# Nineteen projection panels with channels in rows, and a new order of the input projection, in a one-core hybrid decoder layer

## The chip, the cores and the metric

The kernel runs on one core of a Trainium2 chip. TensorE (PE in the profile; its weight loads are a row of their own, PEld) multiplies; VectorE (DVE), ScalarE (ACT) and GpSimd (POOL) do the work on elements; SyncE (SP) issues all transfers. The metric is the time of one execution in microseconds (us) on the device: the median of the runs of a kernel. Lower is better.

## What is computed

One layer over 256 tokens of 1024 channels, all in float32. Cut to what matters here:

```python
h = rms_norm(x, ln1_g)
q, k, v, z, xbc, dt_raw, gate_a, gate_b = split(h @ w_in)      # 1024 x 10272
y_a = attention(rms_norm(q), rms_norm(k), v) @ w_o_attn        # 16 heads of 64, causal
xs, bm, cm = split(silu(conv4(xbc) + conv_b))                  # conv along tokens, per channel
dt = softplus(dt_raw + dt_bias); a = dt * -exp(a_log)          # 32 heads, 4 groups
y = y_diag + y_off + d_skip * xs                               # two chunks of 128 tokens
#   y_diag: (C B^T) * exp(segsum(a)) @ (xs dt);  y_off: (C @ state of chunk 0) * exp(cumsum(a))
y_b = (rms_norm_by_group(y * silu(z)) * ssm_norm_g) @ w_o_ssm
x = x + (sigmoid(gate_a) * y_a + sigmoid(gate_b) * y_b) @ w_out
h2 = rms_norm(x, ln2_g)
g_ff, u_ff = split(h2 @ w_gate_up)
x = x + (silu(g_ff) * u_ff) @ w_down
x = x + (p @ w_ple_proj) * sigmoid(rms_norm(x, ln3_g) @ w_ple_gate)
```

## The kernel before

Every big product runs in *panels* of 512 weight columns by 1024 rows. A panel's weights come in four transfers of 128x1024 (two k rows of 512 columns each) into `raw`; ACT rounds them to `wh` and DVE subtracts to get the rest, `wl` (`split_w`, L260 to L263). The activations are split in the same way into a high and a low part, so a product is three matmuls in the fp32r type: high by `wh`, high by `wl`, low by `wh`.

In a `Panel` (L333) the activations are stationary and the weights move: for each of two token tiles and eight k rows three matmuls of 512 columns (`step`, L365), 48 in all, into two PSUM banks of the tag `g`. The result has tokens in rows. What is used with channels in rows is turned back by PE: `evac_xbc` (L499) and `evac_z` (L533) copy the two banks out with the token's `rstd` as scale and transpose them in eight 128x128 blocks; `evac_gu` and `ff_task` (L1016, L1026) form silu(gate) times up in token rows and transpose four blocks. The activations carry the gain of the norm but not its rstd, which is applied when a panel is copied out.

`dt_task` (L416) forms dt from sixteen small fp32r matmuls and writes the decays; `e1`, the decay from a chunk's start, has tokens in rows. In `ssm_task` (L608) four groups are worked in two halves of four heads: `decay_rows` fills rows by POOL and by transfers on SP (L639, L640), `prep` makes the group's operands, `seg` the decay matrices, `out_` (L681) the products within a chunk, `off` (L697) the product with the state: one F32 matmul of 512 columns, a DVE product with `e1`, and four transposes.

PSUM has four banks `g` for panels and four `b` (`pb`) for all else. The buffers of SBUF are pools: `s4` 26, `s2` 8, `raw` 4, `wh` 3, `wl` 6.

What runs in which order on PE is set by a planner in the program, `Filler` (L78): tasks are generators that yield a due time in ns of planned PE time, from the table `LAG` (L68); after each step of a panel the earliest due task may put its instructions behind it. `queue` (L156) fixes this order on PE. On ACT, DVE and SP the order comes from priorities (`prio`: weights before copies out before background) in a scheduler. `PANELS` (L34) is the order of the input projection; the weights lie in that order in DRAM, and SP loads them in a row.

## Time and profile before

| | us |
|---|---|
| median of 3 runs | 602.09 (601.91 to 602.18) |
| span of the profiled execution | 600.7 |
| PE busy | 593.9 (99%) |
| PE weight loads (beside PE) | 484.6 (81%) |
| DVE busy | 424.1 (71%) |
| ACT busy | 338.6 (56%) |
| POOL busy | 38.7 (6%) |

Busy time of PE is modelled from the records of its pipelined matmuls, so the price of one is read from the distance between starts. The input projection with attention and SSM runs to about 345 us, the output projection and the residual to 395, the eleven gate and up panels to 520, the down projection to 580, the last panels to the end.

### The profile page before, as it was taken

What the parts mean: (1) busy time and instruction counts of PE and PEld (TensorE: products, weight loads), DVE (VectorE), ACT (ScalarE), POOL (GpSimd) and SP (SyncE); (2) the same over time, 40 slices, a digit from 0 to 9 for tenths busy, and PEclk for the clock granted to TensorE, in tenths of its full rate; (3) what the DMA queues carried; (4) which work ended last, traced back from release to release, by engine and by line L of the source; (5) the groups of instructions that cost most, each with busy time, mean ns of one, the idle gap of its engine ahead of it and who ended that gap; (6) DMA issues with size and microseconds to landing.
All of it is one profiled execution on the core that took longest, in us unless ns stands there. A gap on an engine that the chain in (4) does not pass through costs nothing.

```text
span 600.7 us, 8147 instructions
## 1 busy us (share of the span) xinstructions
PE 593.9 (99%) x2965; PEld 484.6 (81%) x2965; DVE 424.1 (71%) x668; ACT 338.6 (56%) x513; POOL 38.7 (6%) x47
## 2 busy tenths in 40 slices
PE   8999999999999999999999999999999999999997
PEld 7888888787777878887787788888888888888886
DVE  5689999978997765677875475756756666646465
ACT  6766666556775545576646444755544544445353
POOL 2000103412010011101000000000000000000000
PEclk9999999999999999999999999999999999999999
DMA  8945644533444445555544475556565555555641
GB/s 278 323 152 175 210 142 142 174 131 117 140 127 149 143 150 170 187 166 160 162 161 164 139 232 188 185 165 208 163 200 188 161 201 187 190 188 182 201 141 70
DMA packets 31192, 103.88 MB, mean 173 GB/s; under 512 B 3568, under 2 KB 4912, under 8 KB 31152
## 3 DMA queue, kind: packets, MB, share of 16 engines
q1 hardware_dynamic: 31152, 103.36, 53.3%
q8 instruction: 23, 0.38, 0.3%
q14 instruction: 17, 0.14, 0.1%
HBM read 102.23 MB, written 1.05 MB: 172 GB/s over the span
## 4 chain that ended last, share of the span: by engine, by line
PE 96%; DVE 1%; DMA 1%; ACT 0%; SPq 0%; issue 0%; ACTq 0%
PE g L170 85%; PE pb L170 6%; PE pb L192 5%; DMA raw<-in_head 1%; SPq L248 0%; DVE s L750 0%; ACT wh L151 0%; DVE s L658 0%; ACT s L151 0%; DVE wl L263 0%; DVE s L785 0%; DVE s L663 0%; DVE s L742 0%; DVE s L1063 0%; DVE s L1064 0%
## 5 line engine op out<-in xcount | busy, mean ns | idle before, releaser
L170 PE MATMUL g<-wh,s 128*128 128x512 f32 (+1 forms) x1508 | 486.7, 395 | 0.6 <-ACT wh L151 0.6
L170 PEld LDWEIGHTS g<-wh,s 128*128 128x128 f32 x1508 | 282.7, 189 | 59.6 <-issue 1.8
L263 DVE TENSOR_TENSOR wl<-raw,wh 128x1024 fp32r<-128x1024 f32 (+2 forms) x193 | 230.4, 1196 | 129.6 <-ACT wh L151 127.0
L151 ACT ACTIVATE wh<-raw 128x1024 fp32r<-128x1024 f32 (+2 forms) x193 | 199.9, 1038 | 177.7 <-PE g L170 149.8
L170 PE MATMUL g<-wl,s 128*128 128x512 f32 (+1 forms) x754 | 294.2, 392 | 0.0
L170 PEld LDWEIGHTS g<-wl,s 128*128 128x128 f32 x754 | 142.1, 189 | 27.8 <-issue 1.0
L151 ACT ACTIVATE s<-pb 128x512 f32<-128x512 f32 (+4 forms) x64 | 33.6, 544 | 30.4 <-PE pb L192 16.1
L192 PEld LDWEIGHTS pb<-ident,s 128*128 128x128 f32 x302 | 37.9, 140 | 11.4 <-issue 0.9
L192 PE MATMUL pb<-ident,s 128*128 128x128 f32 x302 | 47.1, 272 | 0.0
L151 ACT ACTIVATE s<-g,rstd 128x512 f32<-128x512 f32 (+1 forms) x50 | 28.5, 583 | 20.5 <-PE g L170 18.7
L520 DVE SCALAR_TENSOR_TENSOR s<-pb,vecs,s 128x255 f32<-128x255 f32 (+2 forms) x72 | 32.0, 475 | 1.4 <-ACT s L151 1.2
L170 PE MATMUL pb<-s,s 128*64 128x128 f32 (+6 forms) x328 | 32.6, 304 | 0.4 <-ACT s L151 0.4
L151 ACT ACTIVATE s<-pb,vecs 128x256 f32<-128x256 f32 (+2 forms) x48 | 25.9, 550 | 11.1 <-PE pb L192 5.0
L170 PEld LDWEIGHTS pb<-s,s 128*64 128x64 f32 (+2 forms) x328 | 23.1, 154 | 9.9 <-issue 4.7
L381 POOL TENSOR_TENSOR rstd<-tiny,mhalf 128x2 f32<-128x2 f32 x3 | 2.3, 762 | 315.2 <-DVE tiny L380 295.3
L151 ACT ACTIVATE s<-s 128x512 f32<-128x512 f32 (+3 forms) x24 | 19.0, 792 | 4.3 <-DVE s L978 4.0
L571 POOL TENSOR_TENSOR tiny<-tiny,mhalf 128x8 f32<-128x8 f32 x8 | 16.0, 1995 | 73.2 <-DVE tiny L569 73.2
L635 POOL TENSOR_SCALAR_AFFINE_SELECT rr<-a_h 128x512 fp32r<-128x512 f32 x16 | 13.6, 860 | 100.2 <-PE pb L170 61.7
L151 ACT ACTIVATE s<-s,tiny 128x128 f32<-128x128 f32 (+1 forms) x32 | 14.2, 444 | 6.5 <-DVE tiny L788 6.5
L1022 DVE SCALAR_TENSOR_TENSOR s<-g,rstd,s 128x256 f32<-128x256 f32 x22 | 10.6, 481 | 7.5 <-ACT s L151 7.5
L676 DVE TENSOR_TENSOR s<-s,s 128x512 f32<-128x512 f32 x16 | 11.9, 748 | 0.3 <-ACT s L151 0.3
L1023 DVE SCALAR_TENSOR_TENSOR s<-g,rstd,s 128x256 f32<-128x256 f32 x22 | 10.7, 484 | 0.7
(120 smaller groups left out, 235.2 us busy)
## 6 DMA issues: line engine op xcount, KB each, us to landing
raw<-in_w_big SPq DMA_DIRECT2D x176, 512.0 KB
raw<-in_head SPq DMA_DIRECT2D x4, 512.0 KB
s<-in_xk SPq DMA_DIRECT2D x4, 512.0 KB
raw<-in_head SPq DMA_DIRECT2D x7, 256.0 KB
raw<-in_w_pp SPq DMA_DIRECT2D x2, 512.0 KB
raw<-in_w_dn SPq DMA_DIRECT2D x2, 512.0 KB
out<-s SPq DMA_DIRECT2D x3, 256.0 KB
xraw<-in_head SPq DMA_DIRECT2D x2, 256.0 KB
```

The source lines that it names most:

```text
L151: return nc.scalar.activation(o, i, f, **kw)
L170: ins = nc.tensor.matmul(o, lhsT, rhs, start=start, stop=stop).ins
L192: queue(nc.tensor.transpose(o, i, ident[: i.shape[0], : i.shape[0]]).ins, False)
L263: nc.vector.tensor_sub(wl, raw, wh.bitcast(F32))
L381: nc.gpsimd.tensor_tensor(dst, t, mhalf[:, : ss.shape[-1]], op=ALU.pow)
L520: stt(cc[:, sft:], pu[:, j, : T - sft], cw[3 - sft], cc[:, sft:], op0=ALU.mult, op1=ALU.add)
L571: nc.gpsimd.tensor_tensor(f, ms, mhalf, op=ALU.pow)
L635: nc.gpsimd.affine_select(r, bcast(a_h[:, c, h0 : h0 + 4].bitcast(F32), P), pattern=[[0, 4], [1, P]], compare_op=ALU.is_ge, fill=0.0, base ...
L676: nc.vector.tensor_tensor(m, m, cbm[:, g, c].unsqueeze(1).to_broadcast([P, 4, P]), op=ALU.mult)
L1022: stt(t[:, tt], pan.ps[tt][:, :T], r, t[:, tt], op0=ALU.mult, op1=ALU.mult)
L1023: stt(t[:, tt], pan.ps[tt][:, T:], r, t[:, tt], op0=ALU.mult, op1=ALU.mult)
```

## The change

*Rows.* The six xbc panels and the nine gate and up panels from the third on use a new class `Rows`: 128 weight columns are stationary, and the normed activations move. High and low part lie side by side, so `wh` is multiplied with 512 columns (high and low at once) and `wl` with 256 (high). A panel is 32 such pairs into four banks `g`, one for each block of 128 channels; ACT copies a bank and DVE adds its two halves. Channels come out in rows, and the transposes go.

*Narrow.* The four z panels do the same with 256 columns three times, 96 matmuls into two banks, which are read in place.

*Norm.* Both need activations that carry their rstd. `norm_task` spreads rstd over rows by one F32 matmul with `ones_m`, scales x and splits it into `hn`; `norm2` does it for h2. The gate panels `ga` and `gb` use `hn` too.

*dt* becomes eight F32 matmuls of 32 stationary columns that go to four quarters of the array's columns. *Decay by loads:* `e1` is made with heads in rows, stored to DRAM, and loaded back in two transfers, spread over 64 rows each. *off* is four F32 matmuls of 128 columns with channels in rows, one DVE product and one sum, with no transposes. *out_* does eight heads of a group in one run, and all decay rows of the next group are filled at once. The two `pow` of a q or k panel become one. `PANELS` and `LAG` are new; `s4` has 22 buffers, `raw` 5, `wh` 4.

```diff
 PANELS = [
+    v0 v1 q0 q1 k1 k0 gb0 xbc5 xbc4 xbc1 xbc2 xbc3 xbc0 z0 z1 z2 z3 gb1 yb0 ga0 yb2 ga1 yb1 yb3
-    xbc4 xbc0 xbc5 xbc1 xbc2 xbc3 k0 q0 z0 z1 gb0 yb0 yb1 q1 v0 z3 k1 z2 gb1 v1 yb2 yb3 ga1 ga0
...
+    class Rows:
+            self.ps = [psg.tile([P, 512], F32, tag="g", name=nm("gr")) for _ in range(4)]
+        def add_all(self, acts, after):
+            for k0 in range(0, 8, 2):
+                if k0 % 4 == 0:
+                    parts = next_chunk()
+                for b in range(4):
+                    cs = slice(b * P, b * P + P)
+                    for k in (k0, k0 + 1):
+                        (wh, wl), hl_ = parts[k % 4], acts[k]
+                            mm(self.ps[b], wh[:, cs], hl_, k == 0, False, main=True)
+                            mm(self.ps[b][:, :T], wl[:, cs], hl_[:, :T], False, k == 7, main=True)
+                    fill.step()
+                    if k0 == 6:
+                        after(b, self.ps[b])
+    class Narrow:
...
+                        for n, (w, a) in enumerate(((wh, ah), (wh, al), (wl, ah))):
+                                mm(o, w[:, cs], a, k == 0 and n == 0 and b % 2 == 0, k == 7 and n == 2 and b % 2 == 1, main=True)
...
+    def norm_task():
...
+            mm(pr[:, :T], ones_m, dg.rearrange("p a t -> p (a t)"), True, True)
...
     def dt_task():
-                mm(pd[:64, :T], wd[:, k].rearrange("p a h -> p (a h)"), ah, k == 0, k == 7)
+            halves(
+                (pd[32 * (k % 4) : 32 * (k % 4) + 32, :T], wdt[:, k], xr_of(k), k < 4, k >= 4)
+                for k in range(8))
...
-            act(e1, pe[:, 3], AF.Exp)
+            act(e1t[:32], pe1, AF.Exp)
+            nc.sync.dma_start(e1d, e1t[:32])
+            for a in range(2):
+                nc.sync.dma_start(e1c[rows_of[a]], e1d.rearrange("(j a) l -> a j l", a=2)[a : a + 1].to_broadcast([64, 16, P]))
...
+    def rows_xbc(i):
+        def after(b, ps):
+                e = s2([512])
+                act(e, ps)
+                nc.vector.tensor_add(u[:, b], e[:, :T], e[:, T:])
+                act(cc, u[:, b], AF.Identity, scale=cw[3], bias=v[:, V_CB + ct : V_CB + ct + 1])
+                for sft in (1, 2, 3):
+                    stt(cc[:, sft:], u[:, b, : T - sft], cw[3 - sft], cc[:, sft:], op0=ALU.mult, op1=ALU.add)
...
         def off(g):
-                mm(po, cb[:, g], xe, True, True)
+                    mm(po[:, i], xe[:, i * P : i * P + P], cb[:, g], True, True)
+                nc.vector.tensor_mul(yo, po, e1c[:, 4 * g : 4 * g + 4])
-                    transpose(pt_[:, i], yo[:, i * P : i * P + P])
-                nc.vector.tensor_add(y[:, :, P:T], y[:, :, P:T], pt_)
+                nc.vector.tensor_add(y[:, :, P:T], y[:, :, P:T], yo)
...
     for i in range(2, NFF):
-        pan = Panel()
-        evac_gu(i, pan)
+        Rows().add_all(h2n, rows_gu(i))
```

Where it moves instructions is shown at three places. On **PE** in the gate and up stage, before, a token tile takes six matmuls of 512 columns into its bank (`g`) for two k rows, three for each, and transposes that belong to the panel before (`s_847` is its product) stand between:

```order
L170 MATMUL g_4130<-wh_4132,s_758_3663 128x512
L170 MATMUL g_4130<-wl_4133,s_758_3663 128x512
L170 MATMUL g_4130<-wh_4132,s_759_3664 128x512
L170 MATMUL g_4130<-wh_4132,s_758_3663 128x512
L170 MATMUL g_4130<-wl_4133,s_758_3663 128x512
L170 MATMUL g_4130<-wh_4132,s_759_3664 128x512
L192 MATMUL pb_4152<-ident,s_847_4122 128x128 x2
L170 MATMUL g_4129<-wh_4138,s_758_3663 128x512
L170 MATMUL g_4129<-wl_4139,s_758_3663 128x512
```

In the changed kernel a block of 128 channels has its own bank (`gr`), the activation (`s_784`) moves, and 512 and 256 columns take turns:

```order
L170 MATMUL gr_4331<-s_796_4145,wh_4391 128x512
L170 MATMUL gr_4331<-s_796_4145,wl_4392 128x256
L170 MATMUL gr_4440<-s_784_4088,wh_4446 128x512
L170 MATMUL gr_4440<-s_784_4088,wl_4447 128x256
L170 MATMUL gr_4440<-s_784_4088,wh_4446 128x512
L170 MATMUL gr_4440<-s_784_4088,wl_4447 128x256
L170 MATMUL gr_4441<-s_784_4088,wh_4446 128x512
L170 MATMUL gr_4441<-s_784_4088,wl_4447 128x256
L170 MATMUL gr_4441<-s_784_4088,wh_4446 128x512
```

The transposes between are gone, and two k rows of a bank are four matmuls in turns of 512 and 256 columns, where they were six of 512.

On **ACT** at the end of a gate and up panel, before, the two copies out of the banks (`s_864<-g`) each stand between roundings of weights (`wh`):

```order
L151 ACTIVATE s_857_4157<-pb_4152 128x512
L151 ACTIVATE s_864_4211<-g_4129,rstd_3511 128x256
L151 ACTIVATE wh_4227<-raw_4226 128x1024
L151 ACTIVATE wh_4265<-raw_4264 128x1024
L151 ACTIVATE s_864_4211<-g_4130,rstd_3511 128x256
L151 ACTIVATE wh_4271<-raw_4270 128x1024
L151 ACTIVATE wh_4310<-raw_4309 128x1024
```

In the changed kernel the four copies out of the banks `gr_4552` to `gr_4555` come at the panel's end, with one `wh` ahead of the last of them:

```order
L151 ACTIVATE wh_4721<-raw_4720 128x1024
L151 ACTIVATE s_895_4640<-gr_4552 128x512
L151 ACTIVATE s_896_4647<-gr_4553 128x512
L151 ACTIVATE s_897_4654<-gr_4554 128x512
L151 ACTIVATE wh_4727<-raw_4726 128x1024
L151 ACTIVATE s_898_4661<-gr_4555 128x512
L151 ACTIVATE s_910_4685<-s_880_4556 128x512
```

Two copies became four, and the fourth is queued behind a rounding of weights.

On **SP** after the weight loads of the first panels, before, only the decay rows (`rr`) stand between loads (`raw`):

```order
L275 DMA raw_1006<-in_w_big 128x1024
L275 DMA raw_1012<-in_w_big 128x1024
L275 DMA raw_1080<-in_w_big 128x1024
L639 DMA rr_831<-low_h 1x4x128
L639 DMA rr_835<-low_h 1x4x128
L640 DMA rr_831<-low_l 1x4x127
L640 DMA rr_835<-low_l 1x4x127
```

In the changed kernel the decay goes out (`e1d<-e1t`) and comes back (`e1c`, two transfers) ahead of the first decay rows:

```order
L277 DMA raw_1109<-in_w_big 128x1024
L277 DMA raw_1115<-in_w_big 128x1024
L569 DMA e1d<-e1t 32x128
L277 DMA raw_1201<-in_w_big 128x1024
L571 DMA e1c<-e1d 64x16x128 x2
L714 DMA rr_1517<-low_h 1x4x128
L277 DMA raw_1207<-in_w_big 128x1024
L715 DMA rr_1517<-low_l 1x4x127
```

The store and the two loads are new in the queue; the weight loads behind them keep their order.

## Rows read from the trace of the kernel before

**Rows 1.** The page: busy time of the engines, the granted TensorE clock in 40 slices (tenths of full speed), and the chain of work that ended last, by engine and by line.

```profile
PE 593.9 (99%) x2965; PEld 484.6 (81%) x2965; DVE 424.1 (71%) x668; ACT 338.6 (56%) x513; POOL 38.7 (6%) x47
...
PEclk9999999999999999999999999999999999999999
...
PE 96%; DVE 1%; DMA 1%; ACT 0%; SPq 0%; issue 0%; ACTq 0%
PE g L170 85%; PE pb L170 6%; PE pb L192 5%; DMA raw<-in_head 1%; SPq L248 0%; DVE s L750 0%; ACT wh L151 0%; DVE s L658 0%; ACT s L151 0%; DVE wl L263 0%; DVE s L785 0%; DVE s L663 0%; DVE s L742 0%; DVE s L1063 0%; DVE s L1064 0%
```

**Rows 2.** The waits of PE in the whole span, by line and by what was waited for: us in total, times, longest us.

```profile
PE pb L205 <- DVE ones L209: 1.1, 1, 1.1
PE g L170 <- ACT wh L151: 0.6, 1, 0.6
PE pb L170 <- ACT s L151: 0.4, 1, 0.4
PE pb L170 <- DVE s L744: 0.3, 1, 0.3
```

**Rows 3.** The timeline of PE in the gate and up stage (start, duration, instruction, how many in a row; durations overlap), and the busy time of the engines over one panel's period of that stage (PE, PEld, DVE, ACT, POOL, granted clock, DMA).

```profile
434.66 0.39 PE L170 MATMUL g<-wh,s 128*128 128x512 f32 x1
434.89 0.38 PE L192 MATMUL pb<-ident,s 128*128 128x128 f32 x2
435.03 0.48 PE L170 MATMUL g<-wh,s 128*128 128x512 f32 x1
435.34 0.39 PE L170 MATMUL g<-wl,s 128*128 128x512 f32 x1
...
436.27 0.62 PE L170 MATMUL g<-wh,s 128*128 128x512 f32 x2
...
436.95 0.61 PE L170 MATMUL g<-wh,s 128*128 128x512 f32 x2
...
416.83:428.22 11.39, 11.39 (x54) 9.36 (x53) 7.35 (x10) 5.68 (x7) 0.00 (x0) 1.00 0.59 192
```

**Rows 4.** The timeline of PE in a stretch of 256-column matmuls near the end, and the weight loads that belong to `wh` in the main groups, with their count and mean duration (ns, before the second bar).

```profile
594.98 0.40 PE L170 MATMUL pb<-wh,s 128*128 128x256 f32 x2
...
595.34 0.40 PE L170 MATMUL pb<-wh,s 128*128 128x256 f32 x2
...
L170 PEld LDWEIGHTS g<-wh,s 128*128 128x128 f32 x1508 | 282.7, 189 | 59.6 <-issue 1.8 <-ACT wh L151 1.0 <-DVE s L572 0.2
```

**Rows 5.** The timeline of PE around dt (the sixteen records at 27.86), around a run of two-way F32 products (204.50) and around an off step (its two records at 214.83 stand between main matmuls, of which one lies between 214.83 and 215.92).

```profile
27.86 2.04 PE L170 MATMUL pb<-s,s 128*64 128x256 f32 x16
29.73 0.40 PE L170 MATMUL g<-wh,s 128*128 128x512 f32 x1
...
204.50 1.09 PE L170 MATMUL pb<-s,s 128*64 128x128 f32 x16
205.53 0.50 PE L170 MATMUL g<-wl,s 128*128 128x512 f32 x1
...
214.60 0.39 PE L170 MATMUL g<-wh,s 128*128 128x512 f32 x1
214.83 1.02 PE L170 MATMUL pb<-s,s 128*128 128x512 f32 x2
...
215.92 0.40 PE L170 MATMUL g<-wl,s 128*128 128x512 f32 x1
```

**Rows 6.** DVE by groups of line, tile and shape: count, busy us, mean ns, idle time before them.

```profile
L263 DVE TENSOR_TENSOR wl<-raw,wh 128x1024 fp32r<-128x1024 f32 x184 | 224.7, 1223 | 126.4 <-ACT wh L151 123.9
...
L520 DVE SCALAR_TENSOR_TENSOR s<-pb,vecs,s 128x255 f32<-128x255 f32 x24 | 11.2, 475 | 1.2 <-ACT s L151 1.2
...
L1022 DVE SCALAR_TENSOR_TENSOR s<-g,rstd,s 128x256 f32<-128x256 f32 x22 | 10.6, 481 | 7.5 <-ACT s L151 7.5
...
L526 DVE SCALAR_TENSOR_TENSOR s<-s,s 128x1024 f32<-128x1024 f32 x6 | 7.3, 1218 | 0.0
...
L744 DVE TENSOR_TENSOR s<-s 128x256 f32<-128x256 f32 x4 | 1.7, 414 | 0.0
```

**Rows 7.** ACT by groups: count, busy us, mean ns, and the idle time before them with what ended it.

```profile
L151 ACT ACTIVATE wh<-raw 128x1024 fp32r<-128x1024 f32 x184 | 194.7, 1060 | 174.5 <-PE g L170 149.8 <-issue 13.0 <-DVE wl L263 3.3
...
L151 ACT ACTIVATE s<-g,rstd 128x256 f32<-128x256 f32 x23 | 10.7, 466 | 9.5 <-PE g L170 9.5
...
L151 ACT ACTIVATE s<-g 128x512 f32<-128x512 f32 x12 | 7.1, 590 | 2.2 <-PE g L170 1.7 <-PE pb L170 0.5
```

**Rows 8.** Busy time of the engines in stretches of the first part (us; PE, PEld, DVE, ACT, POOL, then granted clock, DMA share and GB/s).

```profile
36.00:60.00 24.00, 24.00 (x114) 19.71 (x113) 22.51 (x53) 16.13 (x23) 0.00 (x0) 1.00 0.50 154
60.00:84.00 24.00, 24.00 (x119) 20.16 (x118) 22.84 (x47) 15.05 (x25) 2.45 (x4) 1.00 0.54 176
84.00:108.00 24.00, 23.96 (x116) 19.42 (x114) 22.28 (x39) 16.72 (x24) 8.05 (x6) 1.00 0.47 148
108.00:132.00 24.00, 23.67 (x133) 18.95 (x134) 21.50 (x33) 12.56 (x17) 6.93 (x5) 1.00 0.47 161
```

**Rows 9.** The waits of SP's DMA queue: us in total, times, longest us.

```profile
SPq L275 <- DVE wl L263: 412.0, 163, 7.1
SPq L639 <- POOL rr L635: 24.6, 9, 6.0
...
SPq L1138 <- DMA out<-s: 1.5, 1, 1.5
```

More of the change, by code (lines that the diff above doesn't have):

```diff
@@ L417, in dt_task @@
         with prio("bg"):
-            wdt_raw = s4([8, 32])
-            nc.sync.dma_start(wdt_raw, w_dt)
-            wd = s4([8, 2, 32], F32R)
-            act(wd[:, :, 0], wdt_raw)
-            nc.vector.tensor_sub(wd[:, :, 1], wdt_raw, wd[:, :, 0].bitcast(F32))
+            wdt = s4([8, 32])
+            nc.sync.dma_start(wdt, w_dt)
+            nc.vector.tensor_tensor(wdt, wdt, bcast(g1, 32), op=ALU.mult)
             nc.vector.tensor_scalar(dsk, v[:, V_DS : V_DS + 16], 0.5, None, op0=ALU.mult)
+        while "norm" not in done:
+            yield fill.now + 500
         yield fill.now + LAG["dt"]
@@ L556, in evac_qk, with rows_z, after, end @@
+    def rows_z(i):
+        zs = s4([4, T])
+        def after(jj, ps):
+            zz = zs[:, 2 * jj : 2 * jj + 2]
+            with prio("ev"):
+                act(zz, ps, AF.Tanh, scale=0.5)
+                stt(zz, zz, 1.0, ps, op0=ALU.add, op1=ALU.mult)
+        def end():
+            yield fill.now + LAG["z.end"]
+            zsT[i] = zs
+        return after, end
     def evac_qk(kind, i, pan):
@@ L906, in tile_layer, with split_t @@
             continue
+        if kind in ("xbc", "z"):
+            after, end = (rows_xbc if kind == "xbc" else rows_z)(i)
+            fill.drain(lambda: "norm" in done)
+            if kind == "z":
+                Narrow().add_all(hn_act, after)
+            else:
+                Rows().add_all(hn_rows, after)
+            fill.spawn(end(), 0)
+            continue
+        norm = kind in ("ga", "gb")
+        if norm:
+            fill.drain(lambda: "norm" in done)
         pan = Panel()
         for hf in range(2):
-            pan.add(next_chunk(), h_act[4 * hf : 4 * hf + 4], last=hf == 1)
+            pan.add(next_chunk(), (hn_act if norm else h_act)[4 * hf : 4 * hf + 4], last=hf == 1)
         evacuate(kind, i, pan)
-    def split_t(toks, scale_cols, const_scale, acts, delay):
+    def split_t(toks, scale_cols, const_scale, acts, delay, tiles=None):
         th = s4([4, T], F32R)
         tl = s4([4, T], F32R)
+        if tiles is not None:
+            tiles.append((th, tl))
         yield fill.now + delay
@@ L1037, in ff_task, with norm2 @@
         ff.extend((fh[:, j], fl[:, j]) for j in range(2))
+    h2n = []
+    def norm2():
+        yield fill.now + LAG["n2"]
+        with prio("bg"):
+            dg = s2([2, P])
+            for tt in range(2):
+                act(dg[:, tt], ident, scale=rstd2[:, tt : tt + 1])
+        yield fill.now + LAG["n2.rows"]
+        with prio("bg"):
+            pr = pb([512])
+            mm(pr[:, :T], ones_m, dg.rearrange("p a t -> p (a t)"), True, True)
+            rbc = s2([T])
+            act(rbc, pr[:, :T])
+        for k in range(0, 8, 2):
+            yield fill.now + LAG["n2.k"]
+            th, tl = (res2.tiles[k // 4][m][:, k % 4 : k % 4 + 2] for m in range(2))
+            with prio("bg"):
+                t = s2([2, T])
+                nc.vector.tensor_add(t, th.bitcast(F32), tl.bitcast(F32))
+                nc.vector.tensor_tensor(t, t, rbc.unsqueeze(1).to_broadcast([P, 2, T]), op=ALU.mult)
+                h = s4([2, 2, T], F32R)
+                act(h[:, :, 0], t)
+                nc.vector.tensor_sub(h[:, :, 1], t, h[:, :, 0].bitcast(F32))
+            h2n.extend(h[:, j].rearrange("p a t -> p (a t)") for j in range(2))
@@ new lines, in rows_gu, with after, end @@
+    def rows_gu(i):
+        gu = s4([4, T])
+        def after(b, ps):
+            with prio("ev"):
+                e = s2([512])
+                act(e, ps)
+                nc.vector.tensor_add(gu[:, b], e[:, :T], e[:, T:])
+            if b == 3:
+                fill.spawn(end(), 0, LAG["gu"])
+        def end():
+            with prio("bg"):
+                f = s2([2, T])
+                act(f, gu[:, 0:2], AF.Sigmoid)
+                nc.vector.tensor_mul(f, f, gu[:, 0:2])
+                nc.vector.tensor_mul(f, f, gu[:, 2:4])
+                f2 = s4([2, 2, T], F32R)
+                fh, fl = f2[:, 0], f2[:, 1]
+                act(fh, f)
+                nc.vector.tensor_sub(fl, f, fh.bitcast(F32))
+            yield fill.now + LAG["ff.end"]
+            ff.extend((fh[:, j], fl[:, j]) for j in range(2))
+        return after
@@ L1039, in tile_layer @@
+    fill.spawn(norm2(), 0)
     pair(res2.acts, evac_gu)
-    h2 = res2.acts[0] + res2.acts[1]
+    fill.drain(lambda: len(h2n) == 8)
     for i in range(2, NFF):
-        pan = Panel()
-        for hf in range(2):
-            pan.add(next_chunk(), h2[4 * hf : 4 * hf + 4], last=hf == 1)
-        evac_gu(i, pan)
+        Rows().add_all(h2n, rows_gu(i))
     res3 = Residual(xin, V_G3, rstd3)
```

280 lines of the change are left out of this document (145 added, 135 removed).

## The prediction

> **What bounds the kernel now.** I read the page first. TensorE (PE) is busy 593.9 of 600.7 us, the chain that ended last lies on it for 96% (85% main matmuls into the g banks, 5% transposes), and it was granted the higher level, 2.4 GHz, in all 40 slices [rows 1]. PE's waits for other engines add up to 2.4 us [rows 2]. So the time is the sum of what PE is given to do, and the prediction is a count of instructions multiplied by prices, unless another engine takes the bound over. The profiled execution has a span of 600.7 against the median of 602.09, so 1.4 us lie outside the span; I sum against the span and add them back.
>
> **Prices on PE.** The mean durations of the grouped view overlap (a matmul of 512 columns is listed with 396 ns), so I take distances between starts. Three main matmuls of 512 columns take 436.95 - 436.27 = 0.68 us, 0.227 each [rows 3]. Three of 256 columns take 595.34 - 594.98 = 0.36, 0.120 each, though each has its own load of 128 columns, of 189 ns mean: the load runs beside the stream [rows 4]. A line through both prices is 0.0133 us + 0.417 ns for each column. Two transposes stand between the matmuls that start at 434.66 and 435.03, and the matmul behind them is still late, the next starts at 435.34: 0.68 for two matmuls and two transposes, less 0.453, is 0.227, or 0.113 for a transpose. Over a whole gate and up panel it is 11.39 - 48 x 0.227 = 0.51 for four, 0.127 each [rows 3]. I take 0.12.
>
> **Panels in rows.** Nine gate and up panels and six xbc panels become 32 pairs of 512 + 256 columns each. A pair is 0.227 + 0.120 = 0.347; a panel is 11.09 instead of 48 x 0.2267 = 10.88, or +0.21, times 15 = +3.1 us. The columns are the same in number (24,576); what is added is 16 matmuls, each at 0.0133. Four z panels become 96 matmuls of 256 columns, 11.52 instead of 10.88, +0.64 each, +2.6 us. Together 432 more main matmuls: **+5.7 us**.
>
> Here a page speaks for a better result. The row gives 13 ns for each matmul beyond its columns, from the difference of the 512 and the 256 stream [rows 3, 4]. The Trainium skill, "TensorE: Matmul & The Clock Gate", section "Back-to-back issue gap", states N/2.4 + 2.5 ns for a single matmul at the fast level; by it the 432 added matmuls would cost an estimated 1.1 us instead of 5.7. The trace has 0.227 where it gives 0.216, so the trace decides.
>
> **Transposes.** Xbc loses 48, z 32, gate and up 36 and the off step 16: 132 x 0.12 = **-15.8 us** (14.9 to 16.8 by the two prices). All of them stood on PE between main matmuls, so all of it is path.
>
> **Small steps on PE.** *Off:* the F32 matmul of 512 columns costs 215.92 - 214.60 - 2 x 0.227 = 0.87 [rows 5]; four of 128 columns have as many columns in all: 0 (between -0.3 and +0.3 for each of four groups by what the row of 128-column products leaves open), I take 0. *dt:* the 16 old matmuls take 29.73 - 27.86 = 1.87 [rows 5]. The eight new F32 ones of 256 columns are 0.43 each by half of the off price, 3.4 in series and 0.87 if four quarters of the array run together. The nearest row is a run of eight two-way F32 products of 128 columns (16 records): 205.53 - 204.50 = 1.03, where 8 x 0.87/4 = 1.74 would be the price in series [rows 5]. Two-way sharing thus gives 0.59; I take 1.2 for four-way, **-0.7** (between -1.0 and +1.5). *Norms:* two F32 matmuls of 256 columns with ones_m, 0.43 each and about 0.08 for a change of kind (the matmul behind two transposes is 0.31 - 0.227 late [rows 3]): **+1.0**. *Heads in one run:* four runs of half products instead of eight: -0.2 (0 to -0.4). Sum: 5.7 - 15.8 + 0 - 0.7 + 1.0 - 0.2 = **-10.0 us**.
>
> **What the other engines get.** A Rows panel is copied out by ACT (four copies of 128x512, 0.59 each by the row of today's twelve) and added up by DVE (four 128x256 adds, 0.414) [rows 6, 7]. In the gate and up stage DVE is busy 7.35 and ACT 5.68 of 11.39 [rows 3], so DVE goes to about 7.35 - 4 x 0.48 + 4 x 0.414 and some for the two products, ACT to about 5.68 + 4 x 0.59 - 2 x 0.47 = 7.1: covered by PE. In the six xbc panels DVE is the tight one. A panel asks of it four wl (1.223), twelve conv steps (0.475) and the last product (1.218), 11.8 us by mean durations; the four adds make it 13.5 [rows 6], against 11.1 us on PE. But mean durations overlap on DVE too: in 36 to 132 us it is shown busy 22.51, 22.84, 22.28 and 21.50 of 24 with PE at 24.0, 24.0, 23.96 and 23.67 [rows 8], so PE lost almost nothing while DVE was 90 to 95% busy. The excess of up to 2.4 us a panel has to be carried by the lead of the split weights: six wl buffers of two k rows are worth 6 x 11.09/4 = 16.6 us of PE. Since v, q and k panels come first and z panels behind, where DVE has half a panel free, I count it as carried.
>
> **SP.** The decay round trip puts three transfers into SP's queue between weight loads. The first waits for e1t, the two others for the first to land, and all weight loads behind them wait too; at the end of the program a wait of SP for a transfer to DRAM is 1.5 us, and SP's waits for the split weights are 412 us in 163, at most 7.1: that is slack [rows 9]. Waits of SP for the decay rows are 24.6 us, up to 6.0 each, and no PE wait came of them [rows 2, 9]. The bound for the new stop is 0 to 6.0 + 2 x 1.5 = 9 us on SP, covered by five raw, four wh and six wl buffers (at 2.77 us each, far over 9). I take 0 on PE. The Trainium skill, "DMA: Bandwidth & Descriptors", section "Where the ~2 µs actually goes", puts a transfer's fixed time near 2 us, most of it the write receipt, heaviest for HBM, with the wait on the issuing sequencer. That speaks against a trip out and back, an estimated 4 us on SP; today's 1.5 us is of the same order, and either lies under the lead.
>
> **New waits.** The banks are the other new thing. A Rows panel uses all four g banks and the next panel wants bank 0 again 3 x 0.695 = 2.09 us after its last matmul. ACT copies three blocks, then a wh of 1.06 that was itself waiting for the panel's last matmuls, then the fourth block: 1.06 + 0.59 and some 0.2 for signals is 1.85 of 2.09. It fits with 0.2 us. The new order also shortens leads in the SSM (with the new order priced as above, the shortest is some 2.5 us, ahead of the second group's out step). I add **+0.9 us** for waits of this kind (0 to 4): 600.7 - 10.0 + 0.9 + 1.4 = **593.0 us**. Its own range is 590 to 597.
>
> **The rivals.**
> - *The copies come late.* If the wh ahead of the fourth copy starts later, each of 15 Rows panels stops for 0.3 to 0.5 us: +4.5 to +7.5, 597 to 600.5. For it: the margin of 0.2 us, and ACT's idle time today mostly ends with a PE matmul, that is, its wh is issued just when PE frees the buffer [rows 7]. Against: a fourth wh buffer. Chance 0.12.
> - *DVE becomes the bound and the time gets slower than before.* In the six xbc panels the price by means holds, 6 x (13.5 - 11.1) = 14.4 us, and the lead of 16.6 is already spent on the norm and dt work of the same stretch. It decides as soon as that other work exceeds about 2 us and wl comes late, so PE waits for DVE: 593 + 14 = 607. For it: DVE is at 95% there today [rows 8]. Against: PE was still full at that level. Chance 0.10.
> - *Loads are exposed.* If the 256-column matmul had to wait for its own load of 189 ns, a pair would be 0.227 + 0.189 = 0.416 and the panels +33 us, 626. The 256-column stream with its own loads speaks against it [rows 4]. Chance 0.02.
> - *Added matmuls are nearly free.* If in the alternating stream the 13 ns vanish behind the longer matmul, the 5.7 fall away and the time is 593.0 - 5.7 = 587.3. Against: neither stream of today shows it [rows 3, 4]. Chance 0.04. The Trainium skill's formula of "TensorE: Matmul & The Clock Gate" comes out near it, an estimated 588.4; by the 0.227 of the trace it does not hold here.
>
> **How the numbers follow.** The forecast has 0.72. The range needs 8 in 10: the forecast's 590 to 597 and the late copies up to 600 hold 0.84, and the bounds of dt, off, transposes and waits lie inside, so 590 to 600. About 0.2% (1.2 us) is what a measurement of this kernel can tell from no change. Faster than 600.9: forecast 0.70, free matmuls 0.04, late copies 0.11, together 0.85; within: 0.05, from the tails of forecast, copies and DVE; slower: 0.10, from DVE and exposed loads.
>
> **What would show it.** In the profile after, a gate and up panel should take 11.1 us of PE and a pair 0.347; a z panel 11.5; transposes 171 instead of 303; PE's waits under 4 us, and no wait for ACT's copies at the start of a Rows panel. The forecast is wrong if PE shows waits for ACT s ahead of gr matmuls (the first rival), for DVE wl or the SSM's products before 210 us (the second), or if pairs are at 0.42 or 0.335 (the third and fourth).

## The result and the profile after

The changed kernel takes 596.45 us (median of 4 runs, 595.75 to 597.93) against 602.13 for the kernel before in the same comparison: a ratio of 0.9911, interval 0.9897 to 0.9925. It is 5.7 us faster, where 9.1 was forecast; 596.45 lies in the range of 590 to 600. The profiled execution took 595.75 us, its span is 593.7, so 2.05 us lie outside the span (2.05 to 2.13 in the four runs); runs of the kernel before that list both have 1.7 outside. The prediction added back 1.4, the median of three runs less the span of another one. Of the 3.45 us between 593.0 and 596.45, then, 2.1 lie in the span of the profiled run (593.7 against 591.6), 0.65 outside it, and 0.7 is the distance of the median from that run, the fastest of the four.

The page of the changed kernel, the same lines as in [rows 1]:

```profile
PE 584.9 (99%) x3293; PEld 498.7 (84%) x3293; DVE 452.4 (76%) x733; ACT 360.3 (61%) x562; POOL 38.8 (7%) x44
...
PEclk9999999999999999999999999999999999999999
...
PE 94%; ACT 2%; DVE 1%; issue 1%; POOL 1%; DMA 1%; SPq 0%
PE g L170 50%; PE gr L170 27%; PE gn L170 8%; PE pb L170 7%; PE pb L192 3%; ACT wh L151 1%; ACT s L151 1%; POOL tiny L644 1%; DMA raw<-in_head 1%; DVE wl L265 0%; SPq L250 0%; DVE s L647 0%; DVE s L1120 0%; DVE tiny L640 0%; DVE s L1107 0%
```

PE is as full as before (99%) at the same clock, with 9 us less of busy time. Its share of the chain fell from 96 to 94%: ACT has 2% of it now. The waits of PE, beside [rows 2]:

```profile
PE pb L205 <- DVE ones L209: 1.1, 1, 1.1
PE pb L192 <- DVE s L1108: 1.0, 1, 1.0
PE pb L170 <- ACT s L151: 0.9, 1, 0.9
PE gr L170 <- ACT s L151: 0.7, 1, 0.7
PE g L170 <- DVE s L647: 0.6, 1, 0.6
```

They are 4.3 us in all instead of 2.4. The wait at line 205 is the start, the same as before. Four are new: g at 50 us (`s L647` is the copy of a q panel, behind the merged pow), gr at 88 us (the first Rows panel wants a bank that the last gate panel's copy still reads), pb at 196 us (attention's values behind the copy of its transposed weights), and pb at 405 us (transposes of the second gate and up panel behind DVE's product).

To see where the forecast lost, I took every PE record from the third panel on, gave each main matmul the price of the prediction (0.2267 or 0.120), and put the rest of each distance down to what stands in it. Main matmuls at these prices: 488.3 us before, 494.1 after, the 5.7 to 5.8 of the forecast; this is the count at the forecast's own prices and tests no price. Beyond them, between two main matmuls with nothing else around: 2.8 before, 4.55 after (+1.75; the pairs of the Rows panels take 2.5 beyond their price and short stops 1.2, while the matmuls of 512 columns in the other panels take 1.0 beyond theirs where they took 2.8). At the groups of small matmuls and transposes and the first matmul behind them, waits included: 77.0 before, 63.3 after (-13.8, where the forecast's terms come to -15.7). The sum is -6.3 of the span's -7.0. The first two panels, whose time depends on the first loads, were 0.6 us faster; this is chance, as the third panel starts at 25.9 us here, at 26.5 before, and between 25.7 and 27.0 in the later runs. So 1.75 us were lost in the bare stream and 1.9 at the small steps, of which the forecast had allowed 0.9 as waits.

**The bare stream.** Two Rows panels with nothing in between, an xbc panel and a gate and up panel, in the view by windows (columns as in [rows 8]); [rows 3] has the panel of before, 11.39:

```profile
123.49:134.59 11.10, 11.10 (x67) 9.79 (x66) 11.07 (x21) 9.13 (x14) 0.00 (x0) 1.00 0.54 173
...
437.64:448.95 11.31, 11.31 (x66) 9.81 (x65) 8.10 (x12) 7.52 (x11) 0.00 (x0) 1.00 0.60 185
```

The first takes the 11.09 of the forecast, the second 11.31. Ten of the fifteen Rows panels have nothing in between: this one has the first price, the eight later gate and up panels have the second, and one xbc panel takes 11.53 with a stop. The timeline of PE in the first (start, duration, instruction):

```profile
123.84 0.39 PE L170 MATMUL gr<-s,wh 128*128 128x512 f32 x1
124.07 0.28 PE L170 MATMUL gr<-s,wl 128*128 128x256 f32 x1
124.19 0.39 PE L170 MATMUL gr<-s,wh 128*128 128x512 f32 x1
124.42 0.28 PE L170 MATMUL gr<-s,wl 128*128 128x256 f32 x1
124.53 0.39 PE L170 MATMUL gr<-s,wh 128*128 128x512 f32 x1
```

124.53 - 123.84 = 0.69 for two pairs, 0.347 each. And in the second:

```profile
440.12 0.40 PE L170 MATMUL gr<-s,wh 128*128 128x512 f32 x1
440.36 0.28 PE L170 MATMUL gr<-s,wl 128*128 128x256 f32 x1
440.47 0.40 PE L170 MATMUL gr<-s,wh 128*128 128x512 f32 x1
440.71 0.28 PE L170 MATMUL gr<-s,wl 128*128 128x256 f32 x1
440.82 0.40 PE L170 MATMUL gr<-s,wh 128*128 128x512 f32 x1
441.06 0.28 PE L170 MATMUL gr<-s,wl 128*128 128x256 f32 x1
441.18 0.40 PE L170 MATMUL gr<-s,wh 128*128 128x512 f32 x1
```

441.18 - 440.12 = 1.06 for three pairs, 0.353 each: the distances between starts go 0.24, 0.11, 0.23 and so on in a cycle of three pairs, with 20 ns more in each cycle. Both are the same instructions at the same granted clock (1.00). The stream goes over from one to the other at short stops: from the slow to the fast at one of 0.3 us at 114 us, from the fast to the slow at one of 0.1 us at 101 us. In e8, below, the stop at the same place left the other spacing behind it: the next panel takes 11.31. Over the 445 undisturbed pairs of the kernel the excess over 0.3467 adds up to 2.4 us.

The stop at 114 us is a late copy, too short for the list of waits. ACT and PE around it:

```profile
112.75 1.08 ACT L151 ACTIVATE wh<-raw 128x1024 fp32r<-128x1024 f32 x1
113.70 0.61 ACT L151 ACTIVATE s<-gr 128x512 f32<-128x512 f32 x1
...
114.37 0.50 PE L170 MATMUL gr<-s,wh 128*128 128x512 f32 x1
```

The Rows panel that begins at 111.96 comes to its fourth bank 2.1 us later, and the fourth copy of the xbc panel before it, behind a `wh`, ends at 114.31. PE loses 0.4 us by it, and 0.1 at the same bank of the panel before (101.81). This is the prediction's first rival at its price, at one seam of two Rows panels; at none of those between gate and up panels does PE stop.

**dt** took 60.19 - 58.87 - 0.227 = 1.09 us where 1.2 was taken ([rows 5] has the old one):

```profile
58.87 0.39 PE L170 MATMUL g<-wh,s 128*128 128x512 f32 x1
...
60.19 0.50 PE L170 MATMUL g<-wh,s 128*128 128x512 f32 x1
```

**DVE and SP.** DVE in the stretches of the xbc panels and behind them, beside [rows 8], and SP's waits beside [rows 9]:

```profile
108.00:132.00 24.00, 23.88 (x139) 20.80 (x138) 23.97 (x43) 19.25 (x29) 0.00 (x0) 1.00 0.57 182
132.00:164.00 32.00, 32.00 (x202) 27.25 (x201) 29.83 (x75) 24.89 (x51) 0.00 (x0) 1.00 0.48 159
164.00:204.00 40.00, 39.14 (x340) 36.38 (x339) 36.69 (x98) 28.46 (x70) 0.00 (x0) 1.00 0.41 132
```

```profile
SPq L277 <- DVE wl L265: 332.6, 131, 9.0
...
SPq L715 <- DMA e1c<-e1d: 1.9, 1, 1.9
SPq L569 <- ACT e1t L151: 1.6, 1, 1.6
```

DVE is busy 23.97 of 24 us, and the 0.12 that PE is idle there is the stop at 114 us, for ACT's copy: the excess was carried. SP waits 1.6 us for e1t, 0.9 for the store and 1.9 for the loads that come back; no wait of PE came of them.

### The profile page after: what moved, and what is told of

It reads as the page before. It is cut to its first block, busy times and chain, and to the rows that moved or that the text cites. A ratio compares the mean times of both kernels' runs of the same rounds, so it can differ in the third digit from the quotient of the medians.

```text
span 593.7 us, 8931 instructions
## 1 busy us (share of the span) xinstructions
PE 584.9 (99%) x3293; PEld 498.7 (84%) x3293; DVE 452.4 (76%) x733; ACT 360.3 (61%) x562; POOL 38.8 (7%) x44
## 3 DMA queue, kind: packets, MB, share of 16 engines
HBM read 103.28 MB, written 1.06 MB: 176 GB/s over the span
## 4 chain that ended last, share of the span: by engine, by line
PE 94%; ACT 2%; DVE 1%; issue 1%; POOL 1%; DMA 1%; SPq 0%
PE g L170 50%; PE gr L170 27%; PE gn L170 8%; PE pb L170 7%; PE pb L192 3%; ACT wh L151 1%; ACT s L151 1%; POOL tiny L644 1%; DMA raw<-in_head 1%; DVE wl L265 0%; SPq L250 0%; DVE s L647 0%; DVE s L1120 0%; DVE tiny L640 0%; DVE s L1107 0%
## 5 line engine op out<-in xcount | busy, mean ns | idle before, releaser
L170 PE MATMUL g<-wh,s 128*128 128x512 f32 (+1 forms) x900 | 283.1, 391 | 0.7 <-DVE s L647 0.6
L170 PEld LDWEIGHTS g<-wh,s 128*128 128x128 f32 x900 | 169.0, 189 | 35.9 <-ACT s L151 0.9
L170 PE MATMUL g<-wl,s 128*128 128x512 f32 (+1 forms) x450 | 173.5, 388 | 0.0
L170 PE MATMUL gr<-s,wh 128*128 128x512 f32 x480 | 171.4, 400 | 0.8 <-ACT s L151 0.7
L170 PE MATMUL gr<-s,wl 128*128 128x256 f32 x480 | 134.9, 281 | 0.0
L170 PEld LDWEIGHTS gr<-s,wh 128*128 128x128 f32 x480 | 90.1, 188 | 22.7 <-ACT s L151 1.5
L170 PEld LDWEIGHTS g<-wl,s 128*128 128x128 f32 x450 | 84.5, 188 | 16.4
L170 PEld LDWEIGHTS gr<-s,wl 128*128 128x128 f32 x480 | 90.7, 189 | 0.3
L170 PE MATMUL gn<-s,wh 128*128 128x256 f32 x256 | 49.0, 288 | 0.0
L170 PEld LDWEIGHTS gn<-s,wh 128*128 128x128 f32 x256 | 40.2, 191 | 1.0 <-issue 0.3
L710 POOL TENSOR_SCALAR_AFFINE_SELECT rr<-a_h 128x512 fp32r<-128x512 f32 x16 | 16.5, 1044 | 143.9 <-PE pb L170 136.7
```

What stands on the lines that cost most here:

```text
L170: ins = nc.tensor.matmul(o, lhsT, rhs, start=start, stop=stop).ins
L710: nc.gpsimd.affine_select(r, bcast(a_h[:, c, h0 : h0 + 4].bitcast(F32), P), pattern=[[0, 4], [1, P]], compare_op=ALU.is_ge, fill=0.0, base ...
```

## The experiments

All times are medians over 4 to 12 runs, each compared with the kernel before on the same chip.

**e1: 512, 512, 256, 256.** The order of the four matmuls of a block's two k rows.

```diff
                     for k in (k0, k0 + 1):
                             mm(self.ps[b], wh[:, cs], hl_, k == 0, False, main=True)
+                    for k in (k0, k0 + 1):
...
                             mm(self.ps[b][:, :T], wl[:, cs], hl_[:, :T], False, k == 7, main=True)
```

> Changed kernel, but in a Rows panel the two matmuls of 512 columns of a block's two k rows come first and the two of 256 behind them (512, 512, 256, 256 instead of 512, 256, 512, 256); nothing is left out. The trace of the changed kernel shows two steady spacings of the same stream: 0.347 us a pair (one xbc panel of 11.09) and 0.353 (all gate and up panels, 11.30; three pairs of 241+120+236+113+233+117 ns). Theory: the extra 20 ns in three pairs come from the turns of unlike lengths. Then a gate and up panel falls to 11.1 and the kernel by 2 to 3 us, to about 594. Rival: a short matmul has to wait for the load of the next one, and two short ones in a row are worse: a panel of 11.5 to 12, the kernel 3 to 8 us slower. Second rival: the spacing has to do with something else in the stream, and the panel stays at 11.3.

594.80 us, ratio 0.9877 (0.9864 to 0.9889), 1.65 less than the changed kernel. A gate and up panel, by windows:

```profile
438.18:449.33 11.15, 11.15 (x67) 9.73 (x65) 8.05 (x12) 7.48 (x11) 0.00 (x0) 1.00 0.56 189
```

11.15 in each of the eight panels with nothing in between, 0.348 a pair. The theory holds in direction; the gain is below its 2 to 3 us, as the panel falls to 11.15 and not to 11.1, and the fast xbc panel (11.09) went to 11.15, too. The first rival (11.5 to 12) and the second (the spacing belongs to something else) fall.

**e2: two pows.** The copies of q and k panels as before.

```diff
-            nc.gpsimd.tensor_tensor(f.rearrange("p a b -> p (a b)"), ms.rearrange("p a b -> p (a b)"), mhalf, op=ALU.pow)
...
+                nc.gpsimd.tensor_tensor(f, ms, mhalf[:, :8], op=ALU.pow)
```

> Changed kernel with the q and k copies out as before the change: one POOL pow for each token tile instead of one for both. Theory: the PE wait of 0.6 us for DVE at line 647 (a g bank that the first k panel wants) is the price of the merged pow, since the first bank is released only after both tiles' sums; with two pows it goes, 0.5 to 1 us faster. Rival: POOL takes 2.0 us for either pow, so two in a row release the second bank later and the wait stays or grows by up to 1 us.

595.39 us, ratio 0.9888 (0.9875 to 0.9901), 1.1 less than the changed kernel. Of its waits of PE:

```profile
PE g L170 <- ACT wh L151: 1.2, 1, 1.2
...
PE g L170 <- DVE s L646: 0.4, 1, 0.4
PE gr L170 <- ACT s L151: 0.2, 1, 0.2
```

The first is new, but at the start, ahead of the edit. The wait for DVE at 50 us is 0.4 instead of 0.6: it did not go. The one of the first Rows panel at 88 us fell from 0.7 to 0.2: DVE's first copy of the last k panel starts at 83.9 us instead of 87.4 and frees its bank earlier. The merged pow, 2.90 us as a median where one for a tile takes 2.1, cost up to 1 us; the intervals of the two kernels overlap, and the waits, 0.7 less, say it better.

**e3: gate and up panels as before.**

```diff
-    fill.spawn(norm2(), 0)
...
-        Rows().add_all(h2n, rows_gu(i))
+        pan = Panel()
...
+            pan.add(next_chunk(), h2[4 * hf : 4 * hf + 4], last=hf == 1)
+        evac_gu(i, pan)
```

> Changed kernel with the nine gate and up panels as before the change (tokens in rows, 48 matmuls of 512, four transposes each) and without the second norm's spreading. By the forecast's prices (pair 0.347) a Rows panel saves 0.30 us, nine save 2.7, less about 0.5 for the norm's matmul: this kernel 2.2 us slower than the changed one. By the spacing seen in the changed kernel (11.30 against 11.39 before) nine panels save 0.8, and the norm's matmul and the 1.2 us stall in the first of them take it back: no difference within 1 us, or this kernel up to 1 us faster.

595.72 us, ratio 0.9886 (0.9872 to 0.9901): 0.7 less than the changed kernel, no difference that can be told. The forecast had 2.2 us more here. Its panel, by windows:

```profile
442.68:454.07 11.39, 11.39 (x53) 9.36 (x52) 7.36 (x9) 5.68 (x7) 0.00 (x0) 1.00 0.54 180
```

11.39 against 11.31 in rows: nine Rows panels save 0.7, and the stop in the first of them (13.28 instead of 11.31, four transposes included) and the second norm take it back. The nine gate and up panels brought nothing.

**e4: z panels as before.**

```diff
-            if kind == "z":
-                Narrow().add_all(hn_act, after)
...
+        norm = kind in ("ga", "gb", "z")
+    evac = {"z": lambda k, i, p: evac_z(i, p), ...
```

> Changed kernel with the four z panels in tokens in rows again (48 matmuls of 512 columns from the normed activations, copied out, eight transposes each). By the forecast's prices a Narrow panel is 11.52 against 10.88 + 8 x 0.12 = 11.84: this kernel 1.3 us slower than the changed one. Rival: the time of that stretch is set by DVE and the SSM's steps, which lose the copies out here: no difference, or 1 us and more slower beyond the 1.3 because ACT and PE get copies and transposes in the stretch where DVE is full.

602.75 us, ratio 1.0005 (0.9995 to 1.0015): 6.3 us slower than the changed kernel, the whole gain of the change and more. The prices give 1.3 of it. The waits of PE in this kernel:

```profile
PE pb L192 <- DVE tiny L878: 1.4, 1, 1.4
PE pb L192 <- DVE s L1131: 1.1, 1, 1.1
PE pb L205 <- DVE ones L209: 1.1, 1, 1.1
PE pb L192 <- DVE tiny L881: 1.0, 1, 1.0
```

The two lines with `tiny` are new (1.4 and 1.0 us): transposes that wait for small steps of attention on DVE. The second is the stop of the first Rows panel, as before. The listed waits between 208 and 237 us are 4.0 us, where the changed kernel has none, and the granted clock is below 1.00 in that stretch (PE, PEld, DVE, ACT, POOL, then the clock):

```profile
208.00:237.00 29.00, 25.62 (x180) 20.91 (x178) 21.72 (x48) 16.57 (x37) 4.32 (x4) 0.94 0.23 76
```

The seven runs with a mean clock of 0.997 take 603.3 us as a median, the five with 1.000 601.4, so some 2 of the 6.3 us come with the lower clock. This is the second half of the rival: the z panels' copies and transposes fall into the stretch of attention and SSM, whose DVE and ACT steps then come late. What Narrow is worth with an order planned for the other form, this run does not tell.

**e5: three repairs together.** e1, e2 and two due times.

```diff
...
-    "tr.val": 0, "ff": 435,
+    "tr.val": 1300, "ff": 4200,
```

> Changed kernel with three repairs together: the 512 and 256 matmuls of two k rows grouped (512, 512, 256, 256), one pow for each token tile of q and k, and two due times later (the transposes of the first two gate and up panels 4.2 us after their copies instead of 0.4; the attention's values 1.3 us after its transposes instead of 0). Theory: the stops are separate and add up: 1.65 (grouping) + 1.1 (pow) + about 1.2 (the stop at 404 us for DVE) + about 0.9 (the stop at 196 us for ACT), 591.5 to 593.0, near the forecast of 593.0 for the change. Rival: a stop only moves to the next late thing (the first two panels' operands behind the second norm, the SSM's products), and the time stays at 594 to 595.

593.97 us, ratio 0.9863 (0.9851 to 0.9876). The gains of e1 and e2 add up (2.5 of 2.75); the due times brought nothing. Two of its waits of PE:

```profile
PE gr L170 <- DVE s L1110: 1.3, 1, 1.3
...
PE pb L170 <- ACT s L151: 0.9, 1, 0.9
```

The stop at 405 us, 1.0 in the list of the changed kernel, is 1.3 and has another form: not the transposes, but a bank `gr` waits for DVE's product at line 1110, which reads the bank of the second gate and up panel. The wait at pb for ACT stayed at 0.9, since the values came to stand behind the same copy again. The rival holds for the due times.

**e6: gate and up in the form of the z panels.**

```diff
-        Rows().add_all(h2n, rows_gu(i))
+        Narrow().add_all(h2n, rows_gu(i))
```

> Changed kernel with the nine gate and up panels in the form of the z panels: 96 matmuls of 256 columns, no halves to add. By 13 ns beyond its columns for each matmul, a panel is 96 x 0.120 = 11.52 against 11.30 now: nine panels and the kernel 1.9 us slower, DVE about 0.3 us less busy for each block. Rival: the 256 stream, too, takes extra time beside other loads; a panel of 11.7 or more and the kernel 4 us slower. Second rival: the price hangs on the turns of unlike lengths alone and like ones run at 0.117 (the short matmul's distance in the fast turns): a panel of 11.2, the kernel 1 us faster.

596.09 us, ratio 0.9899 (0.9886 to 0.9911): the same as the changed kernel. The panel is 11.52, the forecast's price to the digit:

```profile
437.07:448.59 11.52, 11.52 (x98) 11.52 (x97) 6.80 (x7) 6.47 (x9) 0.00 (x0) 1.00 0.55 182
```

Eight panels are 1.7 slower, and the first is 12.23 instead of 13.28, since it takes two banks and not four and the stop at 405 us is gone. PEld is busy in every moment of this panel, so it stays open whether the columns or the loads set the 0.120. Six transposes of 128 columns in the changed kernel, each with its own load and the last of them listed with 0.27 us, follow one another at (0.82 - 0.27)/5 = 0.11:

```profile
195.05 0.82 PE L192 MATMUL pb<-ident,s 128*128 128x128 f32 x6
```

That is near 0.120 with half the columns; no run separates the two.

**e7: more work on DVE.** 24 additions that nobody reads, in the xbc panels.

```diff
+                for _ in range(4):
+                    nc.vector.tensor_add(idle, c[:, 0:2], c[:, 2:4])
                 act(u, c, AF.Tanh, scale=0.5)
```

> Changed kernel with four additions of 128x512 on DVE for each xbc panel that nobody reads, 24 in all, 14.4 us by 0.60 each or 16.5 by the mean duration; nothing of the result is left out. DVE is busy 11.07 of 11.10 us in a panel there in the changed kernel. Theory of the forecast: the lead of the split weights carries DVE's excess, and still has room: under 2 us slower. Rival (the forecast's second): the lead is nearly spent, and what is added shows on PE as waits for DVE: 8 to 15 us slower.

611.65 us, ratio 1.0161 (1.0148 to 1.0174): 15.2 us slower for 14.4 to 16.5 us of work. The wait that took it, and the stretches (PE is the second column, DVE the fourth, the granted clock the one behind POOL):

```profile
PE pb L192 <- DVE s L870: 9.9, 4, 6.1
```

```profile
108.00:132.00 24.00, 23.89 (x140) 20.71 (x139) 24.00 (x43) 19.50 (x28) 0.00 (x0) 1.00 0.52 175
132.00:164.00 32.00, 32.00 (x196) 27.36 (x195) 30.22 (x61) 19.72 (x31) 0.00 (x0) 1.00 0.48 162
164.00:204.00 40.00, 32.86 (x264) 29.81 (x264) 38.08 (x96) 25.56 (x60) 0.00 (x0) 0.87 0.38 130
204.00:240.00 36.00, 31.54 (x265) 27.73 (x266) 32.46 (x78) 22.31 (x60) 5.41 (x6) 0.86 0.14 46
...
191.60:201.60 10.00, 5.97 (x34) 4.14 (x34) 9.63 (x32) 7.15 (x23) 0.00 (x0) 0.50 0.16 52
205.20:215.30 10.10, 6.05 (x34) 4.13 (x34) 7.88 (x22) 6.85 (x22) 0.00 (x0) 0.50 0.01 3
```

PE loses nothing between 108 and 164 us, where the work was put; the split weights are not late. It loses it later, at attention's transposes, which wait for DVE's softmax product (9.9 us in 4 waits, 6.1 from 189 to 195 us). So the rival was right in its price and wrong in its place: DVE has little room from 108 to 204 us, and what it puts off is the background work, not the weights. All listed waits are 15.0 us instead of 4.3, which is 10.7 of the 15.2. The rest stands beside a lower clock: in the stretch of the wait of 6.1 us and the next it is 0.87 and 0.86 as a mean, with two parts of 10 us at 0.50, the 1.2 GHz level, in which PE is busy for 6 us each; in the stretches ahead it is 1.00. How the rest divides is not worked out.

**e8: pools nearer to those of before.**

```diff
-    s4 ... bufs=22 ... raw ... bufs=5 ... wh ... bufs=4
+    s4 ... bufs=24 ... raw ... bufs=4 ... wh ... bufs=3
```

> Changed kernel with pools nearer to those of before: wh 3 and raw 4 buffers instead of 4 and 5, s4 24 instead of 22. It tells whether the copies of a Rows panel are near to being late. With one wh buffer less a rounding of weights waits longer for PE and stands ahead of the fourth copy for longer. Rival of the forecast (late copies): each of 15 Rows panels stops for 0.3 to 0.5 us, 4.5 to 7.5 us slower. Theory: the margin holds, within 1 us of the changed kernel.

600.22 us, ratio 0.9967 (0.9954 to 0.9981), 3.8 slower. But not by the mechanism of the rival: the gate and up panels stay at 11.31, and the one late copy between two xbc panels (114 us) costs 0.45 us instead of 0.4. The waits that came are for weights and for softmax; the 1.2 for `wh` is at the start, as in e2:

```profile
PE g L170 <- DVE wl L265: 2.3, 3, 1.4
PE pb L192 <- DVE s L866: 1.9, 2, 1.6
PE g L170 <- ACT wh L151: 1.2, 1, 1.2
```

So the rival of late copies, as a stop in each Rows panel, falls even with a wh buffer less. The waits for `wl` stand at 248 to 293 us, in the SSM, where the changed kernel has none. Three pools were changed at once; which of them brought the waits is open.

**e9: xbc panels as before, on e8.** It is compared with e8.

```diff
-            if kind == "xbc":
...
-                Rows().add_all(hn_rows, after)
...
+        norm = kind in ("ga", "gb", "xbc")
+    evac = {"xbc": lambda k, i, p: evac_xbc(i, p), ...
```

> The kernel of e8 (pools wh 3, raw 4, s4 24, measured 600.2) with the six xbc panels in tokens in rows again: 48 matmuls of 512 from the normed activations, copied out, eight transposes each; it is to be compared with e8. By the forecast's prices a panel is 10.88 + 8 x 0.12 = 11.84 against 11.09, six are 4.5 us more. By the spacing seen (up to 11.3) it is 3.2 to 4.5. Theory: 3 to 5 us slower than e8. Rival: DVE sets the time in that stretch (11.07 of 11.10 busy), and it has four additions of 0.335 less for each panel here, 8 us in all: no difference or faster than e8.

600.86 us, ratio 0.9983 (0.9974 to 0.9992): 0.6 more than e8, and the intervals overlap. The planner put other small steps between these panels, so panels can't be compared one by one. In the sums of all PE records the small steps cost 4.9 us more than in e8 (68.7 against 63.8; 48 transposes at 0.12 are 5.8), the main matmuls 1.3 less, and the bare stream, waits included, 2.5 less, of which 1.5 are listed waits for `wl` (0.8 against 2.3). With these pools, then, the transposes cost what the forecast says, and most of what xbc in rows saves on PE is given back, as the rival says, though e8's waits for `wl` stand at 248 to 293 us and not among the xbc panels; with the pools of the changed kernel it is open.

**e10: the off step as before.**

```diff
...
-                    mm(po[:, i], xe[:, i * P : i * P + P], cb[:, g], True, True)
...
-                nc.vector.tensor_mul(yo, po, e1c[:, 4 * g : 4 * g + 4])
+                mm(po, cb[:, g], xe, True, True)
...
+                    transpose(pt_[:, i], yo[:, i * P : i * P + P])
```

> Changed kernel with the off step and its decay as before the change: e1 with tokens in rows, no store and loads on SP, one F32 matmul of 512 columns, a DVE product and four transposes for each group. By the forecast's prices: 16 transposes at 0.12, 1.9 us slower than the changed kernel. Rival: the new off waits or the round trip on SP costs as much as the transposes; no difference within 0.7 us.

598.04 us, ratio 0.9941 (0.9929 to 0.9954), 1.6 slower than the changed kernel: the 16 transposes at 0.12 are 1.9. The round trip on SP costs nothing that shows.

**e11: DVE's products ahead of weights, on e5.** The due time of attention's values is 2.2 us here instead of 1.3, too.

```diff
     def evac_gu(_, pan):
-        with prio("ev"):
+        with prio("w"):
```

> The kernel of e5 (593.97) with DVE's products of the first two gate and up panels put ahead of roundings of weights, and the attention's values 2.2 us after its transposes. In e5 the 1.2 us stop at 404 us did not go but moved from the transposes to the third bank of the first Rows panel: a Rows panel takes all four g banks, and two of them are still being read by DVE behind two wl of 1.2 us. Theory: with DVE's order changed that stop goes: 592.5 to 593.0. Rival: the weights become late by what the products take, and the time stays within 0.5 us of 594.

593.99 us, ratio 0.9867 (0.9852 to 0.9882): no difference. The wait of gr is 1.5 us. The product that the bank waits for still comes behind a `wl` and the split of the panel before on DVE (402.72 to 404.45 us), so the edit did not move what it was to move, and says nothing on the theory. The wait of pb for ACT stayed at 0.9.

**e12: a short panel in between, on e5.**

```diff
+    proj(0)
...
     pair(res2.acts, evac_gu)
+    proj(1)
     fill.drain(lambda: len(h2n) == 8)
```

> The kernel of e5 (593.97) with one of the two short panels of w_ple_proj (24 matmuls of 512, 2.7 us by half of 5.58) moved from ahead of the first two gate and up panels to behind them, so that it stands between them and the first Rows panel. Theory: the 1.3 us stop of the third gr bank for DVE comes from a Rows panel's taking all four banks right behind a panel whose two banks are still to be copied out; with 2.7 us in between it goes, 592.5 to 592.9. Rival: the stop has to do with DVE's or ACT's backlog, or the first two gate and up panels now start before their operands are there: 593.5 to 595.

594.82 us, ratio 0.9876 (0.9860 to 0.9893): no gain. Its longest wait of PE:

```profile
PE g L170 <- ACT s L151: 1.4, 1, 1.4
```

The wait of gr is gone (the first Rows panel takes 11.61 instead of 13.50), and a wait of g for ACT's split of the residual, 1.4 us, stands at 375 us, where the moved panel had covered it. So the stop goes with 2.7 us in between, as the theory says, and the time is that of the rival. Since the 2.7 us give DVE time as well as the banks, the run does not part the two.

## Why the prediction came out as it did

*Direction and bound: right.* PE set the time before and after, and a count with prices from distances came near in most terms: 11.09 for a Rows panel, which one of fifteen took, 11.52 for a Narrow panel (e6), 1.9 for 16 transposes of off against 1.6 measured (e10), 1.2 for dt against 1.09, and 171 transposes, as counted.

*The step that was off is the size of a Rows panel.* I took the price of a pair as the sum of two streams that the trace of before shows apart, 0.227 + 0.120. Alternating, they run at 0.353 most of the time, 2.4 us over the 445 undisturbed pairs, and a gate and up panel took 11.31 where 11.1 was forecast. The nine gate and up panels, which were to bring 2.2 net, brought nothing that can be told (e3). The bounds of that term were drawn from the same two rows, so they did not hold the case of a higher price without an exposed load; e1 shows that it is the order of the unlike matmuls, as the grouped order has 0.348; why is open.

*The term for waits was 0.9, and its places were others.* PE's listed waits grew by 1.9. The late copy between two Rows panels, which I thought nearest, came once, 0.4 us at 114 us: the margin of 0.2 took the third copy as done when the panel ends, and there it runs from 112.28 to 112.89. The other stops stand where a Panel turns into a Rows panel and four banks are wanted at once while two are still read (88 us, and 405 us in e5), where one small step is planned right behind another (196 us), and behind a merged pow (50 us). e6, where the first panel takes two banks, and e12 have no stop at 405 us, which speaks for the four banks; in the changed kernel itself the wait listed there is that of transposes for DVE's product, and two `wl` ahead of it on DVE (401.60 to 404.14 us) are not excluded as the cause. Two of the prediction's signs of being wrong were thus in the profile, a wait for ACT ahead of a gr matmul (0.7 us) and 4.3 us of waits where under 4 were expected; neither came near the price of a rival.

*What lies outside the span* was taken as the same before and after. Runs that list both have 1.7 before and 2.05 to 2.13 after. Why the changed kernel has more there is not shown.

*The rule that matmuls are nearly free.* The Trainium skill, "TensorE: Matmul & The Clock Gate", section "Back-to-back issue gap", gives N/2.4 + 2.5 ns for a single matmul. Here like matmuls of 256 columns cost 0.120 in e6, 13 ns more than 256/2.4, and alternating ones more. The trace does not agree. The rival of 587.3 falls by the panels themselves, 11.09 to 11.31 where it asks 10.88.

*The slower rival.* DVE was nearer to the bound than the argument by the lead of the weights said. The lead held, but what it protects is the weights; e7 shows that attention's softmax is what comes late next, 10.7 us of new waits for 14.4 to 16.5 us of work. In the changed kernel itself no wait of PE in 108 to 164 us is put down to DVE.

*What brought the gain* is not the sum of its parts: taking back z costs 6.3 us (some 2 of it with the lower clock), off 1.6, the pools 3.8, gate and up nothing. Each of these was taken back alone under an order and due times made for the whole, so z and the pools carry waits that another order might avoid. How much the new order by itself is worth wasn't measured, nor xbc with the pools of the changed kernel.

The best kernels are e5 and e11, 594.0 us, 2.5 us below the changed kernel, ratio to the kernel before 0.9863 and 0.9867.

## What to carry to other kernels

When two kinds of instruction alternate, don't add the prices that each has in a stream of its own; look for a place where they alternate, and put the case of a higher price into the range. A panel that wants all banks at once met a stop at both places where another kind of panel ends right ahead of it, so look at the seams, and not at the steady state alone. When an engine is full, ask which of its queued work is put off, for the wait appears where that work is wanted, here 25 us behind the end of the xbc panels.

## What the runs showed of the hardware

The same stream of alternating matmuls of 512 and 256 columns has two steady spacings, 0.347 and 0.353 us a pair, at one granted clock (1.00); in the changed kernel it went from one to the other at stops of 0.1 and 0.3 us. In a stream of like matmuls of 256 columns, 0.120 us each, the weight loads are busy all the time (PEld 11.52 of 11.52); which of the two sets the price is open. Eight F32 matmuls of 32 stationary columns on four quarters took 1.09 us, against 8 x 0.43 by half of the off price. In and behind a wait of PE of 6.1 us that ends at 195.5 us (e7), the granted clock was 0.50 in 191.6 to 201.6 and again in 205.2 to 215.3 us, and 1.00 in the stretches ahead.
